# The second block of the gate table gets a buffer of its own, asked for three tiles before the up stage ends; four down weights are split ahead of the gate products

## The chip, the cores and the metric

The kernel runs on one core of one Trainium2 chip. TensorE (PE) multiplies matrices, VectorE (DVE) and ScalarE (ACT) work on elements, GpSimd (POOL) issues the indexed transfers, and SyncE (SP) issues the plain ones. The metric is device time of one execution in microseconds (us), the median of several runs.

## The reference

A two-layer decoder trunk over 256 tokens of width 1024, in float32. Layer 0 mixes by a recurrence, layer 1 by an attention; each layer then runs a feed-forward part of 16384 experts (8 heads, each of which picks 16 experts per token) and a gated embedding. The feed-forward part, cut to what matters here:

```python
# per token: 8 heads x 16 picked experts -> index eidx, gate g (softmax of the scores)
uc  = u_tab[eidx]                # (tokens, 128, 1024)
vc  = v_tab[eidx]
act = gelu(einsum('cd,ckd->ck', x, uc))
out = einsum('ck,ckd->cd', g * act, vc)
```

## The kernel before

**Dense instead of gathered.** For 224 of the 256 tokens the kernel does not gather rows. It multiplies the tokens by the whole table u, 128 tiles of 128 experts each, applies gelu, multiplies by a matrix of gates that is zero where an expert was not picked, and multiplies by the whole table v. The other 32 tokens use gathered rows: POOL fetches 128 rows at a time into `got`, and DVE multiplies and sums them (lines 624 to 630).

**Where the gates come from.** For tokens 0 to 127 the gates are scattered by POOL into a table G in device memory and loaded back in blocks of four tiles (`gt`, 128 x 512, 256 KB; function `gates`, lines 698 to 702). For tokens 128 to 223 they are made on TensorE during the up stage and multiplied into A there (lines 669 to 682, "L681" and "L682").

**Two stages in each layer.** The *up stage* is the loop of lines 756 to 796: for each tile e of u, SP loads it (`raw`, 512 KB, three buffers), ACT rounds it to its high part wH (line 136), DVE subtracts to get the low part wL (line 137), PE makes 24 matrix products (8 column blocks times three products high-high, low-high, high-low; lines 169 to 171) and ACT writes the gelu into column e of A (lines 790, 791). The *down stage* is the loop of lines 804 to 831: for each e, DVE multiplies A's column by the table's gates (line 810), ACT and DVE split the result into aH and aL (line 811), the v tile is fetched and split into wH and wL (line 812), and PE makes 24 products into eight accumulators. Gathered rows go on beside both (line 815).

**What sets the order.** Each engine runs its own instructions in the order in which they stand in its list; a builder puts them there by the program's order and by the dependencies, and `tc.issue_after(i)` holds an instruction until the builder has placed i. `self.lows` is the list of all low-part subtractions recorded so far, so `issue_after(self.lows[-3].ins)` names the third last of them. `fetch` loads and splits a weight tile, and takes it from `self.ready` when `ahead` has fetched it before. Split weights have three buffers (`halves`), raw tiles three (`raws`).

**Buffers of the table blocks.** The first block (tiles 0 to 3) has one buffer in the pool `early`, which exists through the whole feed-forward part; it is asked for at tile 123 of the up loop (line 796). Later blocks live in the pool `late` (line 800, three buffers), which is opened after the up stage's pools are closed and takes their room. The second block is asked for at e = 0 of the down loop (line 806), the third at e = 4 and so on. `self.load` lets SP issue such a load after the last weight tile that was fetched.

Of the kernel before, what the change touches and what calls it, by code (L numbers as in the profile page):

```python
# [8 lines left out]
F32 = mybir.dt.float32  # L9
# [10 lines left out]
P = 128  # L20
# [4 lines left out]
NK = 128  # L25
K = 16
HEADS = 8
TS = 128
# [28 lines left out]
class Trunk:  # L57
# [633 lines left out]
    def peer(self, l):  # L691
        nc, a, V, tc = self.nc, self.a, self.nc.vector, self.tc
        NB, TAIL, NX = 4, 2, 2
        self.side = side = ExitStack()
        with ExitStack() as ph:
            ph.enter_context(self.early_pool)
            early = self.early
            def gates(e):
                pool = late if e else early
                gt = pool.tile([P, NB, TS], F32, tag="gt", name=self.uid("gt"))  # L700
                self.load(gt, self.G[l].rearrange("(p e t) one -> p e (t one)", p=NK, t=TS)[:, e:e + NB])
                return gt

            with ExitStack() as up:
                pool = up.enter_context(tc.tile_pool(name="up", bufs=1, reuse_waits="tile"))
                self.picks = pool.tile([P, 2, HEADS * K, 2], F32, name=self.uid("picks"))
                self.shares = pool.tile([P, 2, HEADS * K], F32, name=self.uid("shares"))
                self.places = pool.tile([P, HEADS * K], I32, name=self.uid("places"))
                stage = up.enter_context(ExitStack())
                rt = stage.enter_context(tc.tile_pool(name="route", bufs=1, reuse_waits="tile"))  # L710
                with self.first_pool:
                    row, r = self.rstd
                    heads = [self.route(l, hd, rt, self.x0, r) for hd in range(NX)]
                    next(heads[0])
                    xs = []
                    for c in range(C):
                        x = self.temp()
                        V.scalar_tensor_tensor(out=x, in0=self.h[c], scalar=self.v(f"norm_ffn{l}", c),
                                               in1=row, op0=ALU.mult, op1=ALU.mult)
                        xs.append(self.split(x, *self.pair(pool, [P, T], f"x{c}")))  # L720
                    for hd in heads[1:]:
                        next(hd)
                self.few = few = ph.enter_context(tc.tile_pool(name="few", bufs=1, side="right", reuse_waits="tile"))
                self.named = [few.tile([P, 2, NG // 2], F32, name=self.uid("named")) for _ in range(2)]
                self.heat = [few.tile([P, NG // 2], F32, name=self.uid("heat")) for _ in range(2)]
                self.xrow = few.tile([P, D], F32, name=self.uid("xrow"))
                acts = ph.enter_context(tc.tile_pool(name="acts", bufs=1, side="right", reuse_waits="tile"))
                A = acts.tile([P, NK, TD], F32, name=self.uid("act"))

                for k in range(2):  # L730
                    ps = self.ps_misc.tile([P, 512], F32, tag="misc", name=self.uid("xrow"))
                    for c in range(4 * k, 4 * k + 4):
                        for x in range(2):
                            nc.tensor.matmul(ps[:GA, c % 4 * P:(c % 4 + 1) * P], lhsT=xs[c][x][:, TD:],
                                             rhs=self.identr, start=c % 4 == 0 and x == 0, stop=x == 1,
                                             skip_group_check=True)
                    nc.scalar.copy(out=self.xrow[:GA, 512 * k:512 * (k + 1)], in_=ps[:GA])
                for g in range(1, GS):
                    nc.gpsimd.dma_start(self.xrow[g * GA:(g + 1) * GA], self.xrow[:GA])
                dense = [(hi[:, :TD], lo[:, :TD]) for hi, lo in xs]  # L740
                while self.cleared[l] < PIECES:
                    self.clear_some(l)
                heads += [self.route(l, hd, rt, xs, None) for hd in range(NX, HEADS)]

                def in_turn():

                    for i, hd in enumerate(heads):
                        for n, _ in enumerate(hd):
                            if n == 3 and NX <= i + 1 < HEADS:
                                next(heads[i + 1])  # L750
                            yield
                pieces = in_turn()
                made, done, begun, ahead = [], 0, None, None
                writes = (i for hd in range(HEADS // 2, HEADS) for i in self.scatter(l, hd))
                rows = self.fetches(l)
                for e in range(NK):
                    if begun is None and e >= 4:
                        for _ in range(1 + e % 2):
                            with tc.issue_after(self.lows[-1].ins):
                                if next(pieces, pieces) is pieces:  # L760
                                    begun = begun or e
                        if begun:
                            stage.close()
                            rt = stage.enter_context(tc.tile_pool(name="hots", bufs=1, reuse_waits="tile"))
                            with tc.issue_after(self.lows[-1].ins):
                                self.turn_picks(rt)
                    bank = self.ps_misc.tile([P, T], F32, tag="misc", name=self.uid("u")) if e % 4 > 1 else None
                    ps = self.lin(f"u{l}", e, dense, bank)

                    if e >= 52 and (e % 4 == 0 if e < 116 else e % 2 == 0):  # L770
                        with tc.issue_after(self.lows[-1].ins):
                            next(rows)
                        if e == 72:
                            with tc.issue_after(self.lows[-1].ins):
                                self.name_rows(1)
                        with tc.issue_after(self.row.ins):
                            for _ in range(4):
                                next(writes, None)
                    if begun:

                        with tc.issue_after(self.lows[-1].ins):
                            for hots in made:
                                self.bank_of_gates(NQ - 1 - done, hots, A, e)
                                done += 1
                            until = min(NQ, NQ * (e - begun + 1) // (NK - 3 - begun))
                            made = [self.hots(rt, NQ - 1 - q) for q in range(done, until)]
                    split = TD - QT * done
                    if done:
                        g = rt.tile([P, TD - TS], F32, tag="gelu", name=self.uid("gelu"), bufs=2)[:, :QT * done]
                        nc.scalar.activation(g, ps[:, split:TD], AF.Gelu_apprx_tanh)  # L790
                    nc.scalar.activation(A[:, e, :split], ps[:, :split], AF.Gelu_apprx_tanh)  # L791
                    if done:
                        V.tensor_tensor(out=A[:, e, split:], in0=g, in1=A[:, e, split:], op=ALU.mult)
                    if e == NK - 5:
                        assert next(writes, None) is None
                        ahead = gates(0)
                assert done == NQ
            acc = [self.ps_acc.tile([P, 2, T], F32, tag=f"acc{i}", name=self.uid("acc")) for i in range(4)]
            proj_pool = side.enter_context(tc.tile_pool(name="proj", bufs=1, reuse_waits="tile"))
            late = ph.enter_context(tc.tile_pool(name="late", bufs=3, reuse_waits="tile"))  # L800
# [2 lines left out]
            self.sums = late.tile([P, D], F32, tag="sums", name=self.uid("sums"), bufs=1)  # L803
            for e in range(NK):
                if e % NB == 0:
                    gt, ahead = ahead, gates(e + NB) if e + NB < NK else None

                gp = early if e < 2 else late
                with tc.issue_after(self.lows[-3].ins):
                    V.tensor_tensor(out=A[:, e, :TS], in0=A[:, e, :TS], in1=gt[:, e % NB], op=ALU.mult)  # L810
                wH, wL = self.split(A[:, e], *self.pair(gp, [P, TD], "a", 2 if e < 2 else None))
# [23 lines left out]
        with ExitStack() as ph:  # L835
            pool = ph.enter_context(tc.tile_pool(name="ple", bufs=1, reuse_waits="tile"))
# [137 lines left out]
```

## Time and profile before

| | |
|---|---|
| median of 3 runs | 1899.68 us (1896.08 to 1904.09) |
| the profiled execution | 1898.7 us |
| its span, first to last instruction | 1897.0 us |
| TensorE busy / weight loads busy | 97% / 95% of the span |
| VectorE / ScalarE / GpSimd busy | 80% / 53% / 39% of the span |
| mean granted TensorE clock | 0.991 of full speed |

The profiled execution lasts 1.7 us longer than its span. The up stage of layer 0 ends at about 536 us and that of layer 1 at about 1498 us. In a timeline row the first number is the start in us from the span's start, the second how long the row's instructions take together, then engine, line, operation, output and inputs, and the count; brackets at the end give the engine's idle time just before and what ended it. Matmuls overlap, so their pace is read from the starts and not from the durations.

### The profile page before, as it was taken

How to read it: one execution, taken by the hardware profiler on the slowest of the kernel's cores; microseconds unless marked ns; L12 is line 12 of the kernel's file. 1: busy time of each engine (PE TensorE's matmuls, PEld its weight loads, DVE VectorE, ACT ScalarE, POOL GpSimd, SP SyncE). 2: the span in 40 equal slices, each digit the busy share in tenths (PEclk: the TensorE clock that was granted, in tenths of full speed). 3: DMA queues.
4: the chain of work that ended last, by engine and by line, in shares of the span. 5: the costliest groups of instructions: out<-in, count | busy, mean ns of one | idle time of the engine just before them, and what ended most of it. 6: DMA issues, size and time to landing. Idle time of an engine off the chain costs nothing.

```text
span 1897.0 us, 40427 instructions
## 1 busy us (share of the span) xinstructions
PE 1834.7 (97%) x15716; PEld 1799.2 (95%) x15716; DVE 1524.5 (80%) x3237; ACT 1006.7 (53%) x1750; POOL 737.0 (39%) x517
## 2 busy tenths in 40 slices
PE   7899999999989999998999999999999899999997
PEld 6799999999989999998887999999999899999997
DVE  6789999888878777776755799998888778777766
ACT  6765555444445545445655655564544445455446
POOL 3216875877412122210200147767885121112102
PEclk9899999999999999999999999999999999999999
DMA  7757777888878888885692467778787788888863
GB/s 255 233 182 194 179 189 215 234 216 222 239 250 305 289 291 283 288 275 182 191 298 66 145 185 184 186 202 235 218 227 215 251 305 285 291 287 288 287 216 103
DMA packets 193394, 435.73 MB, mean 230 GB/s; under 512 B 51568, under 2 KB 87536, under 8 KB 193200
## 3 DMA queue, kind: packets, MB, share of 16 engines
q1 hardware_dynamic: 137104, 365.02, 59.4%
q0 software_dynamic: 56096, 68.12, 15.5%
q8 instruction: 123, 2.02, 0.4%
q14 instruction: 71, 0.58, 0.1%
HBM read 414.25 MB, written 17.96 MB: 228 GB/s over the span
## 4 chain that ended last, share of the span: by engine, by line
PE 78%; DVE 11%; ACT 4%; DMA 3%; issue 3%; POOL 0%; SPq 0%; DVEq 0%; ACTq 0%
PE acc L171 12%; PE acc L170 12%; PE acc L169 12%; PE lin L169 7%; PE lin L170 6%; PE lin L171 6%; DVE wL L137 5%; PE u L171 5%; PE u L169 5%; PE u L170 5%; ACT wH L136 2%; PE gates L677 2%; DMA raw<-u 1%; PE ps_s L493 1%; DMA gt<-G 1%
## 5 line engine op out<-in xcount | busy, mean ns | idle before, releaser
L136 ACT CAST wH<-raw 128x1024 fp32r<-128x1024 f32 x620 | 649.9, 1050 | 624.9 <-PE acc L170 192.6
L137 DVE TENSOR_TENSOR wL<-raw,wH 128x1024 fp32r<-128x1024 f32 x620 | 757.7, 1224 | 255.0 <-ACT wH L136 248.6
L169 PE MATMUL acc<-aH,wH 128*128 128x224 f32 x2048 | 565.4, 276 | 7.7 <-ACT wH L136 7.0
L171 PE MATMUL acc<-aH,wL 128*128 128x224 f32 x2048 | 566.7, 277 | 1.6 <-DVE wL L137 1.6
L170 PE MATMUL acc<-aL,wH 128*128 128x224 f32 x2048 | 563.6, 275 | 1.0 <-DVE aL L137 0.9
L582 POOL DMA_INDIRECT G<-shares,places x256 | 465.9, 1820 | 145.5 <-issue 79.3
L169 PEld LDWEIGHTS acc<-aH,wH 128*128 128x128 f32 x2048 | 395.5, 193 | 8.5 <-ACT wH L136 7.3
L171 PEld LDWEIGHTS acc<-aH,wL 128*128 128x128 f32 x2048 | 395.5, 193 | 1.9 <-DVE wL L137 1.9
L170 PEld LDWEIGHTS acc<-aL,wH 128*128 128x128 f32 x2048 | 395.4, 193 | 1.6 <-DVE aL L137 1.3
L607 POOL DMA_INDIRECT got<-v,named x64 | 98.5, 1538 | 410.8 <-DVE act L810 410.8
L607 POOL DMA_INDIRECT got<-rows,named x64 | 87.3, 1363 | 211.7 <-DVE got L624 132.2
L225 POOL TENSOR_TENSOR tot<-tot,sq 128x256 f32<-128x256 f32 x36 | 30.7, 852 | 265.5 <-ACT sq L223 264.2
L136 ACT CAST aH<-act 128x224 fp32r<-128x224 f32 x256 | 95.4, 375 | 14.9 <-DVE act L810 14.9
L137 DVE TENSOR_TENSOR aL<-act,aH 128x224 fp32r<-128x224 f32 x256 | 98.3, 385 | 0.9 <-ACT aH L136 0.9
L682 ACT COPY act<-gates 128x272 f32<-128x272 f32 (+23 forms) x48 | 13.3, 276 | 144.3 <-DVE act L681 142.0
L810 DVE TENSOR_TENSOR act<-act,gt 128x128 f32<-128x128 f32 x256 | 73.4, 287 | 9.1 <-DMA gt<-G 9.1
L663 DVE SCALAR_TENSOR_TENSOR first<-ints,which,gate 128x256 fp32r<-128x256 f32 x192 | 80.1, 480 | 0.0
L629 DVE SCALAR_TENSOR_TENSOR sums<-got,heat,sums 128x1024 f32<-128x1024 f32 x62 | 79.3, 1280 | 0.0
L624 DVE SCALAR_TENSOR_TENSOR got<-got,xrow 128x1024 f32<-128x1024 f32 x64 | 78.0, 1220 | 0.0
L677 PE MATMUL gates<-first,second 128*128 128x128 f32 x384 | 48.6, 269 | 0.0
L677 PEld LDWEIGHTS gates<-first,second 128*128 128x128 f32 x384 | 46.7, 192 | 0.0
L169 PE MATMUL lin<-x0H,wH 128*128 128x224 f32 (+1 forms) x156 | 44.8, 287 | 0.6 <-ACT act L791 0.6
(907 smaller groups left out, 5149.7 us busy)
## 6 DMA issues: line engine op xcount, KB each, us to landing
raw<-u SPq DMA_DIRECT2D x256, 512.0 KB
raw<-v SPq DMA_DIRECT2D x256, 512.0 KB
G<-zero SPq DMA_DIRECT2D x32, 512.0 KB
raw<-w_q SPq DMA_DIRECT2D x32, 512.0 KB
gt<-G SPq DMA_DIRECT2D x64, 256.0 KB
raw<-w_in SPq DMA_DIRECT2D x16, 512.0 KB
raw<-w_gate SPq DMA_DIRECT2D x16, 512.0 KB
raw<-w_out SPq DMA_DIRECT2D x8, 512.0 KB
```

What stands on the lines that cost most here:

```text
L136: self.copied = self.nc.scalar.copy(out=hi, in_=raw)
L137: self.lows.append(self.nc.vector.tensor_tensor(out=lo, in0=raw, in1=hi.bitcast(F32), op=ALU.subtract))
L169: mm(out, lhsT=sH, rhs=mH, start=start, stop=False, skip_group_check=True)
L170: mm(out, lhsT=sH, rhs=mL, start=False, stop=False, skip_group_check=True)
L171: self.product = mm(out, lhsT=sL, rhs=mH, start=False, stop=stop, skip_group_check=True)
L582: i = nc.gpsimd.indirect_dma_start(out=self.G[l][:, :], out_offset=bass.IndirectOffsetOnAxis(ap=self.places[:, k:k + 1], axis=0), in_=self ...
L607: self.row = self.nc.gpsimd.indirect_dma_start(out=got[:, :], out_offset=None, in_=table, in_offset=bass.IndirectOffsetOnAxis(ap=self.name ...
L624: V.scalar_tensor_tensor(out=row, in0=row, scalar=1.0, in1=self.xrow, op0=ALU.mult, op1=ALU.mult, accum_out=heat[:, i:i + 1])
L629: V.scalar_tensor_tensor(out=self.sums, in0=row, scalar=heat[:, i:i + 1], in1=self.sums, op0=ALU.mult, op1=ALU.add)
L663: V.scalar_tensor_tensor(out=first[:, j], in0=self.ints.unsqueeze(1).to_broadcast([P, 2, NK]), scalar=self.which[:, 0, t:t + 1], in1=self. ...
L677: nc.tensor.matmul(ps[:, j], lhsT=second[:, j], rhs=first[:, j, x], start=j == 0 and x == 0, stop=x == 1, skip_group_check=True)
L810: V.tensor_tensor(out=A[:, e, :TS], in0=A[:, e, :TS], in1=gt[:, e % NB], op=ALU.mult)
```

## The change

The pool `early` gets two buffers for table blocks, and the second block (tiles 4 to 7) uses the second of them. It is asked for at tile 125 of the up loop, two tiles after the first. From the third block on they live in `late` as before, asked for one block ahead. In the down loop, for e = 0 to 3, the v tile is fetched and split ahead of the gate product and the split of A's column, where before it came behind them.

```diff
-                pool = late if e else early
-                gt = pool.tile([P, NB, TS], F32, tag="gt", name=self.uid("gt"))
+                pool, n = (late, None) if e > NB else (early, 2)
+                gt = pool.tile([P, NB, TS], F32, tag="gt", name=self.uid("gt"), bufs=n)
...
-                made, done, begun, ahead = [], 0, None, None
+                made, done, begun, ahead = [], 0, None, []
...
-                    if e == NK - 5:
+                    if e in (NK - 5, NK - 3):
                         assert next(writes, None) is None
-                        ahead = gates(0)
+                        ahead.append(gates(NB * len(ahead)))
...
-                    gt, ahead = ahead, gates(e + NB) if e + NB < NK else None
+                    gt = ahead.pop(0)
+                    if 0 < e < NK - NB:
+                        ahead.append(gates(e + NB))
...
+                if e < 4:
+                    self.ahead(f"v{l}", e)
                 with tc.issue_after(self.lows[-3].ins):
                     V.tensor_tensor(out=A[:, e, :TS], in0=A[:, e, :TS], in1=gt[:, e % NB], op=ALU.mult)
```

Below is SP's list at the end of layer 0's up stage, before. `gt` is a block of the table, `raw<-u` and `raw<-v` are weight tiles; the last two u tiles are raw_7498 and raw_7536, the v tiles 0 to 5 are the last six raws.

```order
L152 DMA gt_7404<-G_145 128x512
L162 DMA raw_7406<-u 128x1024
L162 DMA raw_7451<-u 128x1024
L162 DMA raw_7498<-u 128x1024
L162 DMA raw_7536<-u 128x1024
L162 DMA raw_7590<-v 128x1024
L162 DMA raw_7628<-v 128x1024
L162 DMA raw_7663<-v 128x1024
L162 DMA raw_7701<-v 128x1024
L162 DMA raw_7738<-v 128x1024
L162 DMA raw_7776<-v 128x1024
L152 DMA gt_7583<-G_145 128x512
```

And now, the same place. The last two u tiles are here raw_7500 and raw_7538.

```order
L152 DMA gt_7404<-G_145 128x512
L162 DMA raw_7406<-u 128x1024
L162 DMA raw_7451<-u 128x1024
L152 DMA gt_7497<-G_145 128x512
L162 DMA raw_7500<-u 128x1024
L162 DMA raw_7538<-u 128x1024
L162 DMA raw_7585<-v 128x1024
L162 DMA raw_7623<-v 128x1024
L162 DMA raw_7658<-v 128x1024
L162 DMA raw_7696<-v 128x1024
L162 DMA raw_7738<-v 128x1024
L162 DMA raw_7776<-v 128x1024
```

The second block moved past eight weight loads, from behind v tile 5 to ahead of the last two u tiles; the third block (gt_7731) now follows v tile 5.

DVE's list at the start of layer 0's down stage, before. The v tiles 1, 2 and 3 have the low parts wL_7631, wL_7666 and wL_7704; A's columns 2, 3 and 4 have aL_7660, aL_7698 and aL_7735.

```order
L137 TENSOR_TENSOR wL_7631<-raw_7628,wH_7630 128x1024
L793 TENSOR_TENSOR act_1572<-gelu_7531,act_1572 128x96
L810 TENSOR_TENSOR act_1572<-act_1572,gt_7404 128x128
L137 TENSOR_TENSOR wL_7666<-raw_7663,wH_7665 128x1024
L793 TENSOR_TENSOR act_1572<-gelu_7566,act_1572 128x96
L624 SCALAR_TENSOR_TENSOR got_7529,heat_1567<-got_7529,xrow_1568 128x1024
L137 TENSOR_TENSOR aL_7660<-act_1572,aH_7659 128x224
L137 TENSOR_TENSOR aL_7698<-act_1572,aH_7697 128x224
L810 TENSOR_TENSOR act_1572<-act_1572,gt_7583 128x128
L137 TENSOR_TENSOR aL_7735<-act_1572,aH_7734 128x224
L137 TENSOR_TENSOR wL_7704<-raw_7701,wH_7703 128x1024
```

And now. Line 793 has become 794, and 810 has become 815; v tiles 1, 2 and 3 are wL_7626, wL_7661 and wL_7699, columns 2, 3 and 4 are aL_7666, aL_7704 and aL_7735.

```order
L137 TENSOR_TENSOR wL_7626<-raw_7623,wH_7625 128x1024
L794 TENSOR_TENSOR act_1572<-gelu_7533,act_1572 128x96
L815 TENSOR_TENSOR act_1572<-act_1572,gt_7404 128x128
L137 TENSOR_TENSOR wL_7661<-raw_7658,wH_7660 128x1024
L794 TENSOR_TENSOR act_1572<-gelu_7568,act_1572 128x96
L815 TENSOR_TENSOR act_1572<-act_1572,gt_7404 128x128
L137 TENSOR_TENSOR aL_7666<-act_1572,aH_7665 128x224
L624 SCALAR_TENSOR_TENSOR got_7531,heat_1567<-got_7531,xrow_1568 128x1024
L137 TENSOR_TENSOR aL_7704<-act_1572,aH_7703 128x224
L815 TENSOR_TENSOR act_1572<-act_1572,gt_7497 128x128 x2
L137 TENSOR_TENSOR aL_7735<-act_1572,aH_7734 128x224
L137 TENSOR_TENSOR wL_7699<-raw_7696,wH_7698 128x1024
```

The product with the second block for column 4 stands ahead of v tile 3's low part in both; now the product for column 5 stands there too, and the row product (L624) went from in front of aL of column 2 to behind it. Further up in the same list, L624 went from in front of the last L681 to behind aL of column 0, and the product for column 0 from in front of the low part of u tile 126 to behind the last but one L681.

ACT's list at the same place, as it is now. Columns 2, 3 and 4 are aH_7665, aH_7703 and aH_7734, the v tiles 3, 4 and 5 are wH_7698, wH_7740 and wH_7778.

```order
L136 CAST aH_7665<-act_1572 128x224
L136 CAST aH_7703<-act_1572 128x224
L136 CAST aH_7734<-act_1572 128x224
L136 CAST wH_7698<-raw_7696 128x1024
L136 CAST wH_7740<-raw_7738 128x1024
L136 CAST wH_7778<-raw_7776 128x1024
```

Nothing moved here: before, too, the high part of v tile 3 stood behind the one of A's column 4. Layer 1 has the same moves at its own place. PE's list is the same throughout.

## Rows read from the trace of the kernel before

**Rows 1.** From the page, busy time of the engines: busy us, share of the span, instructions.

```profile
PE 1834.7 (97%) x15716; PEld 1799.2 (95%) x15716; DVE 1524.5 (80%) x3237; ACT 1006.7 (53%) x1750; POOL 737.0 (39%) x517
```

**Rows 2.** Who waited for whom, PE's rows first and then one of DVE, whole span: total us, times, the longest.

```profile
PE acc L169 <- ACT wH L136: 7.0, 2, 3.5
...
PE acc L171 <- DVE wL L137: 1.6, 2, 0.8
...
DVE act L810 <- DMA gt<-G: 9.1, 2, 4.5
```

**Rows 3.** Timeline of PE at the change of stage in layer 0.

```profile
536.08 0.27 PE L171 MATMUL u<-x7H,wL 128*128 128x224 f32 x1
536.74 0.37 PE L169 MATMUL acc<-aH,wH 128*128 128x224 f32 x1 [0.38 <-DVE act L793]
537.16 0.37 PE L170 MATMUL acc<-aL,wH 128*128 128x224 f32 x1
537.37 0.28 PE L171 MATMUL acc<-aH,wL 128*128 128x224 f32 x1
...
545.08 0.28 PE L171 MATMUL acc<-aH,wL 128*128 128x224 f32 x1
548.84 0.37 PE L169 MATMUL acc<-aH,wH 128*128 128x224 f32 x1 [3.49 <-ACT wH L136]
...
550.10 0.56 PE L171 MATMUL acc<-aH,wL 128*128 128x224 f32 x1 [0.78 <-DVE wL L137]
550.45 0.42 PE L169 MATMUL acc<-aH,wH 128*128 128x224 f32 x1
```

**Rows 4.** Timeline of ACT at the same place.

```profile
532.00 1.05 ACT L136 CAST wH<-raw 128x1024 fp32r<-128x1024 f32 x1
...
539.34 0.69 ACT L136 CAST aH<-act 128x224 fp32r<-128x224 f32 x2
547.46 0.38 ACT L136 CAST aH<-act 128x224 fp32r<-128x224 f32 x1 [7.44 <-DVE act L810]
547.75 2.94 ACT L136 CAST wH<-raw 128x1024 fp32r<-128x1024 f32 x3
```

**Rows 5.** Timeline of DVE at the same place.

```profile
535.53 0.67 DVE L681 TENSOR_TENSOR act<-act,gates 128x500 f32<-128x500 f32 x1
536.12 0.28 DVE L810 TENSOR_TENSOR act<-act,gt 128x128 f32<-128x128 f32 x1
...
539.25 0.28 DVE L810 TENSOR_TENSOR act<-act,gt 128x128 f32<-128x128 f32 x1
539.46 1.22 DVE L137 TENSOR_TENSOR wL<-raw,wH 128x1024 fp32r<-128x1024 f32 x1
540.59 0.25 DVE L793 TENSOR_TENSOR act<-gelu,act 128x96 f32<-128x96 f32 x1
540.76 1.22 DVE L624 SCALAR_TENSOR_TENSOR got<-got,xrow 128x1024 f32<-128x1024 f32 x1
...
541.90 0.69 DVE L137 TENSOR_TENSOR aL<-act,aH 128x224 fp32r<-128x224 f32 x2
547.14 0.29 DVE L810 TENSOR_TENSOR act<-act,gt 128x128 f32<-128x128 f32 x1 [4.55 <-DMA gt<-G]
```

**Rows 6.** Timeline of SP's queue: table blocks (`gt`) and weight tiles (`raw`); for several together, the time from the first to the last issue.

```profile
509.88 0.43 SPq L152 DMA_DIRECT2D gt<-G  x1
513.63 9.43 SPq L162 DMA_DIRECT2D raw<-u  x4
527.36 13.67 SPq L162 DMA_DIRECT2D raw<-v  x6
541.08 0.90 SPq L152 DMA_DIRECT2D gt<-G  x2
```

**Rows 7.** Stretches of the span: length, busy time and (count) of PE, PE's weight loads, DVE, ACT and POOL; granted TensorE clock, share of the DMA engines, GB/s.

```profile
513.00:517.00 4.00, 4.00 (x38) 4.00 (x38) 3.90 (x8) 2.48 (x6) 0.34 (x1) 1.00 0.84 277
...
550.45:556.45 6.00, 6.00 (x30) 6.00 (x29) 4.29 (x8) 1.84 (x4) 1.88 (x1) 0.50 0.84 245
1512.58:1515.36 2.78, 2.78 (x15) 2.78 (x14) 2.78 (x5) 0.51 (x2) 0.43 (x1) 0.50 0.75 221
600.00:860.00 260.00, 260.00 (x2330) 260.00 (x2329) 203.87 (x325) 131.15 (x198) 48.04 (x31) 1.00 0.84 284
```

**Rows 8.** Timeline of PE at the change of stage in layer 1: the last u product and the fourth product of v tile 3.

```profile
1498.21 0.27 PE L171 MATMUL u<-x7H,wL 128*128 128x224 f32 x1
...
1512.58 0.41 PE L169 MATMUL acc<-aH,wH 128*128 128x224 f32 x1
```

**Rows 9.** Timelines near the end of layer 0's up stage: ACT's high part of u tile 126, DVE's low part of it, and PE's first product with it.

```profile
524.09 1.05 ACT L136 CAST wH<-raw 128x1024 fp32r<-128x1024 f32 x1 [1.07 <-DMA raw<-u]
...
527.61 1.22 DVE L137 TENSOR_TENSOR wL<-raw,wH 128x1024 fp32r<-128x1024 f32 x1
...
530.79 0.32 PE L169 MATMUL u<-x0H,wH 128*128 128x224 f32 x1
```

**Rows 10.** From the rows of line 152: duration of a semaphore wait on SP (least, median, most, in ns).

```profile
L152 SPq EVENT_SEMAPHORE  x5: 17/17/17, 9.6 to 1836.7; - x5
```

**Rows 11.** Waits of ACT between 500 and 570 us: total us, times, the longest.

```profile
ACT wH L136 <- DMA raw<-v: 1.5, 1, 1.5
```

## The prediction

> **What bounds the kernel now.** I read the page's busy times first: PE works 97% of the span [rows 1], so only what PE waits for, or does slowly, can be saved. The second view is the list of waits. Among PE's, two rows belong to the down products and come twice at the same size: 7.0 us for wH in two waits and 1.6 us for wL in two; and DVE waited 9.1 us in two waits of at most 4.5 for a table block [rows 2]. Two layers, two changes of stage. The third view is the timelines there. PE ends the up stage with the start at 536.08, starts the down products late at 536.74, runs the 72 products of v tiles 0 to 2 until 545.08, and then stands: its next product starts at 548.84, its third at 550.10, its fourth at 550.45 [rows 3].
>
> Reading back from there: PE lacked v tile 3's wH. ACT made that at 547.75, directly behind aH of column 4, for which it had idled 7.44 us [rows 4]. That aH waited for DVE's gate product, which started at 547.14 after 4.55 us of waiting for the second table block [rows 5]. SP had issued that block at 541.08, behind v tile 5 [rows 6], so it landed about 6.0 us after its issue. A weight that PE needed and that depended on no gate stood in line behind one that did.
>
> The fourth view is the granted clock. After this pause PE ran at 0.50, its 1.2 GHz level, from 550.45 to 556.45, and in layer 1 from 1512.58 to 1515.36; in the undisturbed down stage it ran at 1.00 and issued 2330 products in 260 us, one per 0.1116 us [rows 7].
>
> **What the stall costs.** From the last u start to the fourth product of v tile 3 are 76 steps, which at 0.1116 us take 8.48 us. They took 550.45 - 536.08 = 14.37 in layer 0 [rows 3] and 1512.58 - 1498.21 = 14.37 in layer 1 [rows 8]. So 5.89 us are lost in each. Half speed over 6.0 and 2.78 us [rows 7] loses half of each, 3.0 and 1.4. Together 2 x 5.89 + 4.4 = 16.2 us, the most that this change can take from the junctions.
>
> **The change, part by part.**
>
> *The second block is asked for earlier.* In SP's list it now stands behind the raw of u tile 125, that is about 516 us, inside the run of four u loads that begins at 513.63 [rows 6], and it waits for no buffer of the late pool. DVE needs it for column 4 at about 542 (below): 26 us of cover against the 6.0 us that it took when queued behind other loads. The wait of 4.55 us goes in both layers.
>
> Its price: 256 KB more are on the way while u tiles 125 and 126 load. At the 277 GB/s of that stretch [rows 7] this is 0.9 us of transfer, plus an issue of 0.43 on SP [rows 6]. Tile 126 is the tight one: ACT idled 1.07 us for its data and began at 524.09. But DVE did not take it up before 527.61, 2.5 us after ACT's end at 525.1, and PE's first product with it came at 530.79 [rows 9]. So up to about 2 us of lateness is hidden by DVE's other work; beyond that it would show on PE one for one. I take 0. The same bytes leave the later stretch, where v tiles 4 and 5 load.
>
> The Trainium skill, "DMA: Bandwidth & Descriptors", section "Issuing engines are not separate DMA queues", says that transfers started by any engine run on the same 16 DMA engines and interleave; it speaks against asking for more while the u tiles are the last thing to land. Its section "Anatomy of one DMA" gives about 2.0 us plus bytes over 436 GB/s, by which, as an estimate, a block takes 2.6 us. If all of that delayed tile 126, about 0.6 us per layer would show, and the sum would be 1.2 us worse. No run here has shown the delay; the row above bears out only that this tile waits for data.
>
> *Down weights split first, gate product later.* No instruction is added; DVE's list changes. I lay it out again with the steps between starts in its rows: a weight's low part 1.14, a row product 1.14, the last bank of gates 0.59, a gate product 0.20, a gelu product 0.17, a column's low part about 0.30 [rows 5]. ACT's high part of v tile 0 ends at 533.05 as before, since only its data time it [rows 4]. Then: wL 0 from 533.07 to 534.21; gate product 1 and the last L681 to 535.00; about 0.3 for ACT's copy of the last gates, gelu product, about 0.1 for aH; aL 0 at 535.58; row product, aL 1 to 537.32; wL 1 to 538.46; gelu and gate product 2; wL 2 to 539.96; gelu and gate product 3, aL 2 to 540.62; row product, aL 3 to 542.06; gate products 4 and 5 to 542.46. ACT can make aH 4 from 542.37, and wH 3 from 542.66 to 543.71. DVE then makes wL 3 from 543.73 to 544.95.
>
> PE, if it runs without a break, starts its first down product at 536.19; aH 0, aL 0 and both parts of v tile 0 are then there, so the late start goes too. It wants v tile 3's wH 72 steps later, at 544.23 (it is there at 543.71), and its wL at 544.45: 0.5 us late. This is the new last wait: DVE's own backlog. v tile 4's wL ends at about 546.1 against a need at 547.6, and tile 5's at 548.6 against 550.2. So I expect 0.5 us of PE idle per layer where there were 5.89. Waits of 0.38 and 0.78 stand in [rows 3]; after the first the clock did not fall, so I charge no half speed. Bounds: nothing, if DVE gains half a microsecond somewhere, and the present 5.89 with half speed behind it, if DVE or ACT finds a new hold. I take 0.55, near the layout and not the middle, because every duration in it has its row.
>
> *Room.* The early pool grows by 2 KB a partition and other tiles shift. GpSimd's first sum of squares after layer 1's feed-forward now waits for the eight queues that brought table blocks long before: four more waits of 17 ns [rows 10], nothing.
>
> **Sum.** 16.2 - 2 x 0.55 = 15.1 us. Against the profiled execution, 1898.7 (span 1897.0 and 1.7 around it): 1883.6. That execution stands 1.0 below the median of the three runs, 1899.68. I say 1884.
>
> **Rivals.**
>
> *B: a new wait takes most of the place.* DVE has hardly a gap from 533 to 546 in my layout, and wH 3 still stands in ACT's list behind aH 4, which stands behind four row and weight operations of DVE. For it: a row product that finds its gathered row late, or v tiles 3 to 6 landing late (ACT did idle 1.5 us for a v tile there [rows 11]), holds everything by its own length. Against: the rows for these products are asked for 7 us or more ahead, and the issue of v tile 3 hangs on wL 0, which now ends a little earlier. If PE idles 2.5 us per layer and its clock falls as now, the gain is 2 x (5.89 - 2.5) = 6.8: 1892. Without the fall it is 11.2: 1887.5.
>
> *C: it does not do what it says.* The second block is late all the same, or its wait is hidden and weights end last with the same stall: 1897 to 1901. Against: no wait stands on the block's load, and the stall is one chain whose every link is in the rows.
>
> *D: slower.* The extra block delays u tiles 125 to 127 so that PE starves at the end of the up stage; all that follows shifts, and the clock falls there too. The place is PE's product at 530.79; it shows from a delay of 2 us. A delay as long as the block's own 6.0 us costs 4 us and then 1.4 to 3.0 of half speed, 5.4 to 7.0 per layer, still less than the 7.55 saved. With 2.2 for the clock on average, all of the gain (7.55 per layer) is gone from a delay of about 7.4 us, and at about 12 us in each layer the time is 1908 or more. The nearest row is a wait of 1.07 us [rows 9], a tenth of that.
>
> **How the numbers follow.** About 0.5% (9.5 us) is what a measurement of this kernel can tell from no change, so faster means below about 1890. The forecast (1882 to 1887) 0.70; B 0.17, three fifths of it below 1890; C 0.10, where nothing can be told; D 0.03. Faster 0.70 + 0.10 = 0.80, same 0.07 + 0.10 = 0.17, slower 0.03. Range: at the low end the whole 16.2 goes and the run lies as far below the median as the best before (3.6): about 1880. At the high end it takes in B with its fall of clock, 1892, and a microsecond of spread: 1893.
>
> **What would show it.** Right: no DVE wait for a table block; SP's second block issued near 516; the wait of down products for wH below 1 us in both layers; the granted clock at 1.00 through both junctions; 0.3 to 1 us of wait for wL at the fourth v tile. Wrong: PE idle over 2 us between v tiles 2 and 7, a stretch at 0.50 behind it, or PE waiting for u tiles 125 to 127.

## The result, and the profile after

| | before | after |
|---|---|---|
| median of 5 runs each | 1898.60 us | 1889.09 us (1886.99 to 1890.40) |
| profiled execution, its span | 1898.7, 1897.0 us | 1889.44, 1887.7 us |

The ratio is 0.9944, 95% interval 0.9927 to 0.9962. The kernel became faster by 9.5 us; 15.1 had been worked out. The time lies in the predicted range, but 5.6 us of the gain are missing. A later comparison beside other runs of before gave 0.9933 [0.9911, 0.9955]. A gain of 15.1 us would be a ratio of 0.9920: the first interval leaves it out, the second holds it, so the size of what is missing is not sharp.

Busy times hardly moved, as the page's first part says (compare [rows 1]):

```profile
PE 1832.9 (97%) x15716; PEld 1796.4 (95%) x15716; DVE 1523.0 (81%) x3237; ACT 1007.0 (53%) x1750; POOL 741.2 (39%) x517
```

SP issued the second table block at 513.12 us, between u loads, and its six v loads from 524.99 on with no block behind them before the third (its queue, as in [rows 6]):

```profile
513.12 0.51 SPq L152 DMA_DIRECT2D gt<-G  x1
517.37 3.31 SPq L162 DMA_DIRECT2D raw<-u  x2
524.99 13.44 SPq L162 DMA_DIRECT2D raw<-v  x6
538.48 0.42 SPq L152 DMA_DIRECT2D gt<-G  x1
```

At the change of stage the new timeline is what the prediction laid out. PE in layer 0, from the last u product on, as in [rows 3]:

```profile
533.71 0.28 PE L171 MATMUL u<-x7H,wL 128*128 128x224 f32 x1
...
542.18 0.27 PE L170 MATMUL acc<-aL,wH 128*128 128x224 f32 x1
543.07 0.37 PE L171 MATMUL acc<-aH,wL 128*128 128x224 f32 x1 [0.62 <-DVE wL L137]
543.28 0.28 PE L169 MATMUL acc<-aH,wH 128*128 128x224 f32 x1
```

The fourth product of v tile 3 starts 9.57 us after the last u product, where 14.37 had passed. The first down product follows at once, and the one wait left is for wL of v tile 3. In layer 1 the same wait is shorter:

```profile
1500.66 0.37 PE L171 MATMUL acc<-aH,wL 128*128 128x224 f32 x1 [0.28 <-DVE wL L137]
```

PE's waits over the whole span, and then stretches with the columns of [rows 7], show the rest. No DVE row for a table block is left, and the granted clock is 1.00 through both changes of stage (the junctions). But a row stands there that was small before (0.9 us, once): PE waits six times, 3.6 us in all, for the low part of a column of A.

```profile
PE proj L169 <- ACT wH L136: 4.3, 1, 4.3
PE acc L170 <- DVE aL L137: 3.6, 6, 0.9
PE proj L171 <- DVE wL L137: 1.2, 2, 0.8
PE acc L171 <- DVE wL L137: 0.9, 2, 0.6
```

```profile
540.00:560.00 20.00, 19.38 (x173) 19.20 (x173) 16.02 (x29) 10.65 (x16) 6.69 (x4) 1.00 0.93 323
1500.00:1520.00 20.00, 19.72 (x177) 19.54 (x176) 17.35 (x30) 9.60 (x15) 6.39 (x4) 1.00 0.94 327
```

Two of those six, in the timeline of PE at v tiles 18 and 22 of layer 0 (the six stand at tiles 12 to 22):

```profile
584.52 0.37 PE L170 MATMUL acc<-aL,wH 128*128 128x224 f32 x1 [0.56 <-DVE aL L137]
...
596.73 0.37 PE L170 MATMUL acc<-aL,wH 128*128 128x224 f32 x1 [0.91 <-DVE aL L137]
```

**A table of losses.** In every profile I took the starts of the 3072 down products of a layer and charged each block of 96 (four v tiles) with what it lasted beyond 96 x 0.1115 us. The first column adds how late the first down product started. The last block holds 1.8 us in both kernels, for the products of line 826; it is left out, and told of where it differs. In us, layer 0 / layer 1:

| kernel | start and tiles 0 to 3 | 4 to 11 | 12 to 23 |
|---|---|---|---|
| before | 8.05 / 7.35 | 0.76 / 0.03 | 0.11 / 1.28 |
| after | 1.10 / 0.56 | 0.03 / 0.03 | 2.91 / 3.99 |

So the junction (the first two columns) gave 7.7 and 6.8 us, 14.5 in all (predicted 15.1), and v tiles 12 to 23 took 2.8 and 2.7 back. The down stages, from the last u start to the last down product, went from 353.64 and 353.38 to 348.76 and 349.31 us: 8.95 together, of the 9.3 by which the spans differ.

Why there, 40 us behind the change? ACT's waits between 545 and 600 us, first before, then after:

```profile
ACT wH L136 <- PE acc L170: 20.7, 13, 4.0
...
ACT wH L136 <- DMA raw<-v: 3.1, 2, 1.6
```

```profile
ACT wH L136 <- DMA raw<-v: 23.9, 11, 3.6
```

Before, ACT mostly waited for PE to give back a split buffer: the weights were ahead, since they had gone on loading while PE stood and ran at half speed. After, ACT waits for the v tiles themselves. In this part a row step stands at every second v tile (line 818), from tile 20 on at every third, and from tile 24 on nothing is lost.

The longest of the six waits, at tile 22, has a second source. Ahead of that tile ACT waits for DVE's row product to make the last gelu of the rows, and then loads a table (layer 0, after):

```profile
592.54 0.22 ACT L632 ACTIVATE heat<-heat 128x16 f32<-128x16 f32 x1 [2.64 <-DVE got L624]
592.77 1.28 ACT L218 ACT_TABLE_LOAD   x1
594.07 1.05 ACT L136 CAST wH<-raw 128x1024 fp32r<-128x1024 f32 x1
```

Tile 22 lost 1.27 us in each layer; the kernel before, in this profile, loses 1.23 there in layer 1 and next to nothing in tiles 12 to 21.

Three theories for it. *L, the loop of a raw buffer*: a raw buffer is asked for again when DVE has made its low part. The tile lands about 5.2 us later (the medians between 545 and 600 us, and at the same place in layer 1, are 5.0 and 5.1), ACT needs 1.05 and DVE 1.14. Three buffers allow 3 x 2.675 = 8.03 us, so 0.6 are left, and a row product (1.14) on DVE, or a landing slowed by a gather, uses them up. SP's own waits between 545 and 600 us fit it: nearly all are for DVE. (The row names aL; by the starts, each v load left SP 0.03 us after DVE ended the low part of the v tile three before.)

```profile
SPq L162 <- DVE aL L137: 46.2, 20, 4.7
SPq L162 <- DMA raw<-v: 4.8, 5, 2.0
```

That view alone decides nothing: in the run raws4_early below, where tiles 12 to 23 lose nothing, SP waits 49.6 us for DVE. What a turn lasts, from the issue of a load to the end of its low part, says more. Over tiles 12 to 23 it lasted 8.6 and 9.0 us on average, over tiles 24 to 35 7.7. In the kernel before it lasted 8.3 and 8.6 over tiles 12 to 23, also more than 8.03.

*B, bytes*: 1.7 MB in two v tiles (two weight tiles, half a table block, 512 KB of rows), 318 GB/s, is more than the memory gives. *V, the order*: DVE's and ACT's lists hold each other up, whatever lands when.

### The profile page after: what moved, and what is told of

The parts are those of the page before. It is cut to its first block, busy times and chain, and to the rows that moved or that the text cites. A ratio compares the mean times of both kernels' runs of the same rounds, so it can differ in the third digit from the quotient of the medians.

```text
span 1887.7 us, 40429 instructions
## 1 busy us (share of the span) xinstructions
PE 1832.9 (97%) x15716; PEld 1796.4 (95%) x15716; DVE 1523.0 (81%) x3237; ACT 1007.0 (53%) x1750; POOL 741.2 (39%) x517
## 5 line engine op out<-in xcount | busy, mean ns | idle before, releaser
L582 POOL DMA_INDIRECT G<-shares,places x256 | 471.9, 1843 | 149.3 <-issue 81.7
L607 POOL DMA_INDIRECT got<-v,named x64 | 92.2, 1441 | 416.9 <-DVE act L815 416.9
L607 POOL DMA_INDIRECT got<-rows,named x64 | 92.1, 1440 | 187.8 <-DVE got L624 112.9
L624 DVE SCALAR_TENSOR_TENSOR got<-got,xrow 128x1024 f32<-128x1024 f32 x64 | 77.9, 1216 | 0.0
```

The lines of the kernel that those rows point to most:

```text
L582: i = nc.gpsimd.indirect_dma_start(out=self.G[l][:, :], out_offset=bass.IndirectOffsetOnAxis(ap=self.places[:, k:k + 1], axis=0), in_=self ...
L607: self.row = self.nc.gpsimd.indirect_dma_start(out=got[:, :], out_offset=None, in_=table, in_offset=bass.IndirectOffsetOnAxis(ap=self.name ...
L624: V.scalar_tensor_tensor(out=row, in0=row, scalar=1.0, in1=self.xrow, op0=ALU.mult, op1=ALU.mult, accum_out=heat[:, i:i + 1])
```

## The experiments

Every ratio is to the kernel before, timed in the same comparison (medians of before there: 1901.1, 1902.1 and 1902.6).

**A fourth raw buffer.** (label raws4)

```diff
-tail.append((e, self.fetch(f"v{l}", e), (wH, wL)))
+tail.append((e, self.fetch(f"v{l}", e, raws=late if e >= 4 and e % 4 == 3 else None), (wH, wL)))
```

> The changed kernel, with every fourth v tile from tile 7 on loaded into a raw buffer of its own in the pool late, so that four raw buffers stand behind the down loop instead of three. Measure: what PE loses against 0.1115 us per product in v tiles 12 to 23 (changed kernel: 2.9 us in layer 0, 4.0 in layer 1), and the median against 1889.1. Theory L (the loop of a raw buffer: it is asked for again when DVE has made the low part, lands 5.2 us later, then 1.05 of ACT and 1.14 of DVE; three buffers allow 3 x 2.675 = 8.03 us, so 0.6 us are left for a row product or an ACT wait): the loop may now last 10.7 us, the loss falls below 1 us per layer, time 1883 to 1886, ratio to the kernel before 0.992 to 0.993. Theory B (bytes: weights, table and rows ask for about 318 GB/s, more than lands): the same bytes, the loss stays at 2.5 us or more per layer, time 1888 to 1890. Theory V (DVE and ACT are late by their own order): no change, 1888 to 1890.

Ratio 0.9913 [0.9894, 0.9932], median 1885.9. The loss of tiles 12 to 23 is gone, 0.10 / 0.11, with every byte still loaded, and ACT's and DVE's lists are the same there as in the changed kernel; B and V fall. But tiles 4 to 11 lost 1.13 / 0.76, and the last block 0.6 / 1.0 more than its 1.8: the extra buffer let tile 7's load go ahead of tile 6's.

**Fewer gathers.** (half_gather)

```diff
-got.append(self.fetch_row(...))
+got.append(got[-1] if k in (24, 26, 28, 30) else self.fetch_row(...))
```

> The changed kernel without the gathers of rows 24, 26, 28 and 30 (of 0 to 63) in each layer: the row product of each uses the buffer of the row before it again, so these rows are left out of the computation and DVE's list is the same. Four times 512 KB less are loaded beside v tiles 2 to 16. Theory B: the demand falls from 318 to about 270 GB/s, the loss of v tiles 12 to 23 (2.9 and 4.0 us) goes but for about 1 us around the last gelu of the rows, time 1884 to 1886. Theory L: landings become shorter by about 0.5 us, the loss about halves, 1886 to 1888. Theory V: the loss stays, 1888 to 1890.

Ratio 0.9915 [0.9895, 0.9936]. Loss of tiles 12 to 23: 0.10 / 0.13. L had expected half of it to stay. DVE's and ACT's lists are the same as in the changed kernel, and without those gathers a turn lasts 8.0 us in both layers, which PE's pace allows. The medians of the landings do not settle why: a v tile took 4.8 us against 5.0 in layer 0, but 5.2 against 5.1 in layer 1. By this run alone B would stand; it is the run above that refutes it.

**Shorter row products.** (short_rows)

```diff
+w = 64 if 21 <= j <= 30 else D
-V.scalar_tensor_tensor(out=row, in0=row, ..., in1=self.xrow, ...
+V.scalar_tensor_tensor(out=row[:, :w], in0=row[:, :w], ..., in1=self.xrow[:, :w], ...
```

> The changed kernel with the row products 21 to 30 of each layer cut to the first 64 of 1024 columns: that part of the products is left out, the gathers stay. DVE is relieved of about 1 us in each second v tile from 2 to 18. Theory B: the bytes are the same, the loss of v tiles 12 to 23 stays at 2.5 us or more per layer, 1888 to 1890. Theory L: a microsecond less in each second loop of a buffer, the loss about halves or goes, 1884 to 1887. Theory V: the loss goes, 1884 to 1886.

Ratio 0.9939 [0.9919, 0.9958]. Loss of tiles 12 to 23: 2.23 / 0.63, together 2.9 where the changed kernel has 6.9. Neither B (2.5 or more in each layer) nor V (nothing) fits both layers. L's half fits the sum, but layer 0 lost 2.23 of 2.91. The second profile of the changed kernel (below) lost 2.15 / 1.72, so an effect of the row products clear of the spread is not shown here. Nor does the time show one: its interval holds the ratio of the changed kernel.

**Row steps at every third tile throughout.** (thirds)

```diff
-if e % 2 == 0 if e < 20 else e % 3 == 0:
+if e % 3 == 0:
```

> The changed kernel with a row step at every third v tile all through the down loop, where the first twenty tiles had one at every second. The sums of rows then end at v tile 126 instead of 117. Both the bytes (318 to 286 GB/s) and DVE's work in the first twenty tiles fall. Theories B, L and V: the loss of v tiles 12 to 23 goes, less than 1 us per layer is left (the last gelu of the rows moves to tile 30, where it may still cost up to 0.9), time 1883 to 1886. Against all three: the loss stays, and time is 1888 or more, or the end of the down loop waits for the sums (over 1 us of PE waiting behind the last products).

Ratio 0.9958 [0.9943, 0.9973]: no better than the change itself, though the loss of tiles 12 to 23 is 0.05 / 0.05. The end took it: the last row step now comes at tile 126. PE there, and two stretches right behind:

```profile
875.19 3.15 PE L826 MATMUL acc<-sel,sums 128*128 128x32 f32 x16 [2.08 <-DVE sums L629]
```

```profile
875.20:878.00 2.80, 2.80 (x16) 2.80 (x16) 2.50 (x3) 1.05 (x1) 0.00 (x0) 0.59 0.77 208
878.00:885.00 7.00, 7.00 (x45) 7.00 (x45) 2.94 (x8) 2.83 (x8) 1.07 (x2) 0.68 0.44 140
```

2.08 us of waiting, and the clock at 0.59 and 0.68 behind it costs 0.41 x 2.8 + 0.32 x 7.0 = 3.4 more: 5.5, as the last block's loss of 7.4 against 1.8 says, in each layer.

**The parts of the change alone.** block_only leaves out the two lines with `self.ahead`; order_only adds these two lines, and nothing else, to the kernel before.

> The change's first part alone: the second table block has its own room and is asked for at u tile 125; the v tiles 0 to 3 are fetched and split behind the gate products as in the kernel before. Theory 1 (the stall was the late block, and the order adds nothing): PE's wait for wH at v tile 3 goes, the loss in v tiles 0 to 3 falls from 7.5 and 6.8 to 1 to 2 us, the clock stays at 1.00, the lead is lost in tiles 12 to 23 as in the changed kernel, ratio 0.994 to 0.996. Rival 2 (both parts are needed, since DVE's gate products still stand ahead of the weights): the loss stays at 4 us or more per layer, ratio 0.997 to 0.999.

> The change's second part alone: v tiles 0 to 3 are fetched and split ahead of the gate products; the second block is asked for at the start of the down stage as before. Theory 1: the products with the second block still stand ahead of v tile 3's low part in DVE's list, so DVE waits about 4.5 us, PE stands 3 us or more and the clock falls: loss of v tiles 0 to 3 at 6 to 8 us per layer, only the late start (0.55 us per layer) goes, ratio 0.998 to 1.000. Rival 2: the early split carries PE over the late block, the loss falls below 4 us per layer, ratio 0.995 to 0.997.

block_only: 0.9941 [0.9926, 0.9957]; losses at the start and tiles 0 to 3 1.18 / 1.12, tiles 4 to 11 1.58 / 0.55, tiles 12 to 23 2.56 / 3.19. order_only: 0.9994 [0.9982, 1.0005]; 7.57 / 6.32 in tiles 0 to 3, 0.26 / 2.24 in tiles 12 to 23, and DVE's wait stands as in [rows 2]:

```profile
DVE act L812 <- DMA gt<-G: 8.0, 2, 4.3
```

Within what the times can tell, the early block is the whole gain. The early split takes away the late start (0.59 and 0.54 us in block_only, 0 after), but v tile 3 then loses 0.88 and 0.54 us, where it loses 0.16 in block_only. So little is left of it at the junction, and the time can't tell it. Whether the 1.58 us of tiles 4 to 11 come from its absence, one profile can't say.

**The fourth buffer where nothing overtakes.** (raws4_early: as the first diff, with `late if 6 <= e <= 122 and e % 4 == 2 else None`)

> The changed kernel with the fourth raw buffer given to v tiles 6, 10, 14 up to 122 (in the run of tiles 7, 11 up to 127, tile 7's load went ahead of tile 6's, and PE lost 1.1 and 0.7 us in tiles 4 to 7 and 0.6 and 1.0 us more in the last four). Theory L: the loss of tiles 12 to 23 stays away, and the 0.8 to 1.6 us per layer of that run go too: 1882 to 1885 where before takes 1898.6, ratio 0.989 to 0.992. Rival: the four buffers only shift the loss, 0.5 us or more per layer show up elsewhere in the down loop, ratio 0.992 or more.

Ratio 0.9886 [0.9868, 0.9904], median 1879.6: faster than both kernels. Losses 1.45 / 0.84, 0.03 / 0.03, 0.11 / 0.11. ACT now takes a v tile every 2.68 us, PE's pace, as its timeline shows (`issue` marks a wait whose end the profile puts down to nothing). Between 545 and 600 us it waits 3.0 us for loads, where 23.9 stand above:

```profile
574.44 1.05 ACT L136 CAST wH<-raw 128x1024 fp32r<-128x1024 f32 x1 [1.35 <-issue]
575.39 0.38 ACT L136 CAST aH<-act 128x224 fp32r<-128x224 f32 x1
577.12 1.05 ACT L136 CAST wH<-raw 128x1024 fp32r<-128x1024 f32 x1 [1.35 <-issue]
```

```profile
ACT wH L136 <- DMA raw<-v: 3.0, 2, 2.2
```

And the DMA engines move more than in the changed kernel (stretches, after first, then this run):

```profile
546.00:567.00 21.00, 21.00 (x191) 21.00 (x190) 17.82 (x33) 10.59 (x16) 7.20 (x5) 1.00 0.91 317
567.00:590.00 23.00, 22.26 (x196) 21.83 (x195) 16.54 (x31) 10.51 (x16) 7.24 (x4) 1.00 0.88 288
```

```profile
546.00:567.00 21.00, 21.00 (x190) 21.00 (x190) 18.30 (x34) 11.24 (x17) 7.99 (x5) 1.00 0.99 368
567.00:590.00 23.00, 23.00 (x208) 23.00 (x208) 18.33 (x33) 11.06 (x18) 6.46 (x4) 1.00 0.92 320
```

Something else went too. Behind layer 0's down loop PE waits 4.25 us for the second projection tile, and runs at half clock after it; with the fourth buffer that wait is absent and the clock stays up. The kernel before has the wait too (4.3 us), so it is no part of what the change lost. After, and then this run: the timeline of PE, and a stretch that begins 0.6 and 1.3 us behind the second tile's first product:

```profile
887.36 0.58 PE L169 MATMUL proj<-pH,wH 128*128 128x256 f32 x1 [4.25 <-ACT wH L136]
...
888.00:891.80 3.80, 3.33 (x16) 3.18 (x16) 3.71 (x6) 2.12 (x6) 0.80 (x1) 0.50 0.49 146
```

```profile
879.51 0.39 PE L169 MATMUL proj<-pH,wH 128*128 128x256 f32 x1
...
880.80:884.60 3.80, 3.80 (x30) 3.71 (x31) 3.18 (x6) 3.40 (x12) 0.89 (x2) 1.00 0.61 161
```

The buffer's turn is not what did this. The edit also moved two high parts in ACT's list behind the loop, those of the second projection tile and of the first gate tile. In the changed kernel they stand behind six parts of the next stage's input (x0H to x5H), here ahead of the first. All four runs with a fourth buffer have this move. ACT after, and then in this run:

```profile
880.36 0.51 ACT L203 ACTIVATE x0H<-h,vec 128x256 fp32r<-128x256 f32 x1 [1.62 <-DVE h L270]
...
886.28 1.98 ACT L136 CAST wH<-raw 128x1024 fp32r<-128x1024 f32 x2
```

```profile
878.41 1.99 ACT L136 CAST wH<-raw 128x1024 fp32r<-128x1024 f32 x2 [3.36 <-PE acc L170]
880.31 0.50 ACT L203 ACTIVATE x0H<-h,vec 128x256 fp32r<-128x256 f32 x1
```

So the 10.4 us by which the two spans differ are not all the ring's: the down stages account for 6.1, the stretch between them for 2.0.

**The fourth buffer on the kernel before.** (raws4_on_before, the same edit)

> The kernel before, with the same fourth raw buffer for v tiles 6, 10, 14 up to 122. In the kernel before, the stall and the half clock let the loads get ahead, so PE loses only 0.1 us (layer 0) and 1.3 us (layer 1) in v tiles 12 to 23. Theory L: the buffer is worth what is lost there, 0 to 1.5 us, since the stall hid the short loop: ratio 0.999 to 1.000, and the loss of the stall itself stays at 6.5 to 8 us per layer. Rival: the fourth buffer is worth 5 us by itself, whatever stands before it: ratio 0.997 or less.

Ratio 0.9960 [0.9946, 0.9975], 7.6 us: L's 0 to 1.5 us was wrong and the rival's number right, but not as "whatever stands before it". In the profile the loss of tiles 12 to 23 is 0.11 / 0.11, the projection's wait is gone here as well, and the stretch from the last down product of layer 0 to the last u product of layer 1 takes 607.1 us (608.5 and 610.3 in the two profiles of before). Over all profiles this stretch took 606.3 to 608.2 us in the four with a fourth buffer and 608.4 to 612.3 in the nine without. The junction lost 6.55 / 7.44, as L expected. I had left out that wait, and taken one profile's 0.11 and 1.28 for what before always loses.

This kernel and raws4_early were timed in the same comparison, have the same ring and the same order behind the loop, and differ by the change alone: 1893.5 and 1879.6 us. With loads that keep up, the change is worth 13.9 us, close to the 15.1 of the sum.

**Both kernels once more.**

> The changed kernel itself once more, on the chip and beside the runs of the kernel before that the next run shares, for a second profile of where it loses. Theory L: the loss of v tiles 12 to 23 is there again, 2.5 to 4.5 us per layer, as is the wait of 4.3 us for the second projection tile behind layer 0's down loop; ratio 0.993 to 0.996. Rival: the loss was an accident of one execution, under 1 us per layer now, and the ratio is still 0.994, so that the gain was lost elsewhere.

> The kernel before once more, for a second profile. Both theories expect the stall of 14.37 us over the 76 steps at the change of stage in each layer, to 0.5 us. The loss in v tiles 8 to 31 was 0.1 and 1.3 us in the first profile. Theory L (the short loop of three raw buffers is there too and only hidden by the lead that the stall gives): it varies with what the stall was, 0 to 2.5 us per layer. Rival: it is below 0.2 us in both layers, so the gain of 7.6 us from the fourth buffer on the kernel before has its cause outside the down loop.

after_again: 0.9933 [0.9911, 0.9955]; 1.08 / 1.11, then 0.47 / 0.03, then 2.15 / 1.72; the projection waits 4.5 us. The place of the loss repeats, its size is smaller, below the 2.5 that L expected. before_again (1899.7 us): 9.01 / 8.05, then 0.03 / 0.49, then 1.70 / 0.11. So before loses there too, now in the other layer: the loop of three is short in both kernels, and the stall hid most of it. In tiles 12 to 23 the changed kernel loses 5.5 us more than before in the first pair of profiles, 2.1 in the second.

**Row steps two tiles later.** (rows_later: raws4_early, and)

```diff
-if e % 2 == 0 if e < 20 else e % 3 == 0:
+if e >= 4 and (e % 2 == 0 if e < 24 else e % 3 == 0):
```

> The changed kernel with the fourth raw buffer at tiles 6 to 122 and, besides, the row steps of the down loop at even tiles 4 to 22 instead of 0 to 18, then every third tile from 24: two row products of 1.2 us are taken out of DVE's list ahead of v tile 3. Theory 1 (what is left at the change of stage, 0.6 us of waiting for v tile 3's low part and 1.3 and 0.8 us of loss in tiles 0 to 3, is DVE's backlog): the wait falls below 0.2 us and the loss below 0.5 us per layer, time 0.5 to 1.5 us below the run without it (ratio 0.986 to 0.990). Rival 2 (ACT or the load of v tile 3 ends last there): the wait stays at 0.4 us or more.

Ratio 0.9875 [0.9856, 0.9895], median 1879.1. The junction loses nothing: 0.02 / 0.02 in tiles 0 to 3, and PE's list of waits has no row of a down product any more. The wait that was left for v tile 3's low part was DVE's backlog. Each down stage takes 344.88 us. Against raws4_early the interval can't tell the times apart; the down stages are 1.4 and 0.8 us shorter in the profiles.

## Why the prediction was right, and where it was too large

**What the stall costs (16.2 us):** right. The stall was the late block; block_only shows it, and half speed went with it. The table of losses gives the same cost: 8.05 + 0.76 in layer 0 and 7.35 + 0.03 in layer 1.

**The second block asked for earlier, at no cost to the u tiles:** right. Between 505 and 530 us ACT waited 1.4 us for a u tile, once, where [rows 9] has 1.07:

```profile
ACT wH L136 <- DMA raw<-u: 1.4, 1, 1.4
...
PE lin L171 <- DVE wL L137: 0.3, 1, 0.3
```

PE's wait there is 0.3 us, 0.5 before. The last twelve u tiles took 36.2 us in both layers of this profile and 36.9 and 37.0 in the second one; before took 36.4 and 36.2, then 36.2 and 37.0. So no cost stands clear of the spread, and rival D did not come. The 1.2 us were an estimate from the Trainium skill, "DMA: Bandwidth & Descriptors", section "Anatomy of one DMA", whose fit was measured on transfers that GpSimd issues. SP issues these blocks, which took 5.5 us in the median to land where the fit gives 2.6, and the charge did not show on PE.

**Down weights split first (0.55 us left per layer):** right in place, too small in size. PE waited 0.62 and 0.28 us for v tile 3's wL; with the longer steps right around it the loss was 1.10 and 0.56, and 1.08 and 1.11 in the second profile. rows_later shows the named cause. This part of the change brought the late start and little else.

**Sum (15.1 us):** this is the step that failed. It ended at the fourth v tile and let all behind it move forward unchanged. The lead of the weights over PE was made by the stall itself, and with the stall it went. The raw loop, too slow in tiles 12 to 23 (8.6 and 9.0 us a turn against 8.03), then set the pace there, for 5.5 us in the first profile (2.8 and 2.7 over before) and 2.1 in the second. With a fourth buffer on both sides the change gave 13.9 us. Rival B named the mechanism, v tiles landing late, but put it at tiles 3 to 6 and at 2.5 us per layer with or without a fall of the clock. Without the fall it gave 1887.5, nearer to the 1889.1 measured than the forecast of 1884. The clue was in the trace of before: one turn of a raw buffer took 8.3 and 8.6 us there in tiles 12 to 23, more than the 8.03 that PE's pace allows, and still ACT waited for PE (20.7 us between 545 and 600). So the loads were ahead because PE was late. I never asked whether they could have kept up otherwise. That the loop is the cause is shown by the fourth buffer; that the gathers help to overrun it, by half_gather. The part of the row products is argued from DVE's list; short_rows does not show it.

## What to carry to other kernels

When a stall goes, ask what had got ahead because of it, and whether the loads behind can keep up without that lead. For each ring of buffers compare its number times the pace of the consumer with one full turn (landing, each engine that reads it, and what stands ahead of those in their lists): here 8.03 us against 7.4 with nothing beside it, and against 8.6 and 9.0 measured with rows and gathers. The fourth buffer brought about as much again as the change, part of it by moving ACT's list somewhere else: compare the lists of all engines before a gain is put down to the edit. A load that is spread thinner must still end somewhere: the row steps moved out of the busy part cost 5.6 us per layer at the end of the loop.

## What was not expected of the hardware

In 21 us of raws4_early 368 GB/s were moved at a DMA share of 0.99, where the changed kernel moved 317: the rate seen under load is no limit until more is asked for. A wait of 2.08 us by PE was followed by a clock of 0.59 in the next 2.8 us, one of 4.25 us by 0.50; after 0.91 us, in the changed kernel, products followed at one per 0.11 us. And executions vary ahead of the change: in the thirteen profiles, whose code is alike up to u tile 123, the last u product of layer 0 started between 532.6 and 537.2 us, so that a single profile's span says little on 2 us, while the stretches inside it do.
